# A hybrid encoder layer: opening a second pool of split weights 20 steps into the Q projections

## The chip, the cores and the metric

The kernel runs on one core of a Trainium2 chip. The metric is device time in microseconds (us) for one execution. Five engines matter here: TensorE (PE in the profile, with its weight loads as PEld), VectorE (DVE), ScalarE (ACT), GpSimd (POOL) and SyncE (SP), which issues the DMAs that load weights from device memory.

## The reference

One layer of a bidirectional hybrid encoder over 512 tokens of width 2048, all in float32:

```python
h = rms_norm(x, norm_w)
proj = jnp.einsum('bsd,de->bse', h, w_in)
q, k, v, g_attn, xr, g_lru = jnp.split(proj, SPLITS, axis=-1)
attn_out = attention_group(q, k, v, q_norm_w, k_norm_w)      # 8 heads, 2 KV heads, RoPE, softmax
lru_out = lru_group(xr, conv_w, conv_b, ...)                 # conv, two gates, scans in both directions
mixed = jnp.concatenate([rms_norm(attn_out, attn_norm_w) * jax.nn.silu(g_attn),
                         rms_norm(lru_out, lru_norm_w) * jax.nn.silu(g_lru)], axis=-1)
return x + jnp.einsum('bse,ed->bsd', mixed, w_out)
```

The input projection has 4608 columns: q 1024, k and v 256 each, the attention gate 1024, the LRU input 1024 and the LRU gate 1024.

## The kernel before, in words

**How a projection is done.** A product keeps float32 accuracy by splitting both operands into a high and a low half in a rounded float32 type; `mm3` (L143 to L145) then does three matmuls: high by high, high by low, low by high. The activations `x` are split once at the start and stay. The weights come in *chunks* of 256 rows by 512 columns: one DMA (L192) loads a chunk into a `wr` tile (three buffers), and `wsplit` makes of each 128-row half a pair `wh` (a cast on ACT, L203) and `wl` (a subtraction on DVE, L204). A block of 512 columns takes 8 chunks. In each chunk the projection walks over four output tiles, and each of these four *steps* issues 6 matmuls, 3 for each half of the chunk; so a chunk is 24 matmuls and a block is 32 steps. The Q projections are two such blocks, token-major (`proj_tok`), accumulating in four PSUM tiles `pj`.

**Where the split weights lie.** Pool `xw` always holds four `wh` and four `wl` tiles, two chunks' worth. Where a second pool `wx` is open, it holds four more of each, and `wsplit` alternates:

```python
turn_of[0] += k
pool = pools["wx" if "wx" in pools and turn_of[0] % 2 else "xw"]
```

Since `k` is the half of the chunk (0 or 1), the halves go `xw`, `wx`, then `wx`, `xw`, and so on. A pool that is opened takes space of a pool closed before it, and a tile in it waits for the last use of the old tiles that lay there (`reuse_waits="tile"`). Pools `qkv` and `wx` are opened on the right side just after `lru` was closed there, so they lie on memory of the last LRU tiles.

**The stages around the change.** The LRU projections come first, then the K and V projection, which runs while the second half of the LRU work (`lru_half(1, a2)`, four blocks in two pairs) is done on ACT and DVE. The tail of each pair is a chain: tanh (L421), exp (L427), square root (L431) on ACT; then L434, L435, four scans (L438) and two sums (L443) on DVE. After that the program closes `lru`, opens `rot`, `qkv` and `wx`, and issues the two Q blocks, woven with `kv`: the norm and RoPE of `k` (L491 to L505), the split of `v`, the LRU squares (L448 to L453), the two transposed splits of `k` (`kt`), and the LRU's row scale (L635 on).

**What sets the order.** PE's order is the order in which the code is written (a manual schedule). `weave` runs the generator `kv` and lets the projection advance by as many steps as `kv` yields. The other engines' orders are set by a list scheduler at build time; weight loads and splits have a high priority there (`AHEAD`). On the chip each engine takes its own list in that order.

Of the kernel before, what the change touches and what calls it, by code (L numbers as in the profile page):

```python
# [55 lines left out]
def hybrid_kernel(  # L56
# [27 lines left out]
    def opened(name, side):  # L84
        pools[name] = tc.alloc_tile_pool(name=name, bufs=1, side=side, reuse_waits="tile")
        order[side].append(name)
        return pools[name]
# [18 lines left out]
    def nm(s):  # L106
        cnt[0] += 1
        return f"{s}_{cnt[0]}"
# [30 lines left out]
    def f(ap):  # L139
        return ap.bitcast(F32)  # L140
# [120 lines left out]
    def rows(dst, col, dg):  # L261

        for t in range(NT):
            nc.vector.tensor_scalar(dg[:, t, :], ident, col[:, t : t + 1], None, op0=ALU.mult)
        pb = mm()
        nc.tensor.matmul(pb, ones, dg.rearrange("p t q -> p (t q)"), start=True, stop=True)  # L266
        nc.vector.tensor_copy(dst, pb)
# [177 lines left out]
    def lru_squares():  # L445

        hsum = pools["rot"].tile([P, 2, SEQ], F32, tag="hsum", name="hsum")
        nc.scalar.activation(hsum, hp[0], AF.Square)  # L448
        for pair in hp[1:]:
            yield 2  # L450
            sq = pools["rot"].tile([P, 2, SEQ], F32, tag="hsq", bufs=1, name=nm("hsq"))
            nc.scalar.activation(sq, pair, AF.Square)
            nc.vector.tensor_add(hsum, hsum, sq)  # L453
        sums["l"] = [hsum[:, k, :] for k in range(2)]
# [28 lines left out]
    def norm_rope(es, nh, tab):  # L483

        es = [e[:, : nh * HD].rearrange("p (h d) -> p h d", d=HD) for e in es]
        rs = []
        for e in es:
            r = pools["rot"].tile([P, nh], F32, tag=f"rr{nh}", bufs=NT, name=nm("rr"))
            for h in range(nh):
                sq = pools["rot"].tile([P, HD], F32, tag="sh", bufs=1, name=nm("sh"))  # L490
                nc.scalar.activation(sq, e[:, h, :], AF.Square, accum_out=r[:, h : h + 1])  # L491
            rsqrt_mean(r, r, HD, nh)
            rs.append(r)
        for t, (e, r) in enumerate(zip(es, rs)):
            sq = pools["rot"].tile([P, nh, HD], F32, tag="sq", bufs=2, name=nm("sq"))
            nc.vector.tensor_mul(e, e, r[:, :, None].broadcast_to([P, nh, HD]))
            for s in range(2):
                nc.vector.tensor_mul(
                    sq.rearrange("p h (a s d) -> p h a s d", s=2, d=32)[:, :, :, s, :],
                    e.rearrange("p h (a s d) -> p h a s d", s=2, d=32)[:, :, :, 1 - s, :],  # L500
                    tab[:, t, 1, :].rearrange("p (a s d) -> p a s d", s=2, d=32)[:, None, :, s, :]
                    .broadcast_to([P, nh, 2, 32]),
                )
            nc.vector.tensor_mul(e, e, tab[:, t, 0, :][:, None, :].broadcast_to([P, nh, HD]))
            nc.vector.tensor_add(e, e, sq)  # L505
        return es
# [5 lines left out]
    def turn(rot, h):  # L512

        pt = mm()
        for t in range(NT):
            nc.tensor.transpose(pt[:, t * P : (t + 1) * P], rot[t][:, h, :], ident)  # L516
        return pt

    def split_ps(pt, hi, lo):
        nc.scalar.copy(hi, pt)  # L520
        nc.vector.tensor_sub(lo, pt, f(hi))

    def kv(es):
        rot = norm_rope(es, NKV, rk)
        yield 16
        for t in range(NT):
            vv = es[t][:, NKV * HD :]
            vt = pools["qkv"].tile([P, 2, NKV * HD], F32R, tag="v", bufs=NT, name=nm("v"))
            vh[t], vl[t] = vt[:, 0, :], vt[:, 1, :]
            nc.scalar.copy(vh[t], vv)  # L530
            nc.vector.tensor_sub(vl[t], vv, f(vh[t]))
        yield from lru_squares()
        for h in range(NKV):
            yield (20, 4)[h]
            kt = pools["qkv"].tile([P, 2, SEQ], F32R, tag="kt", bufs=NKV, name=nm("kt"))
            kth[h], ktl[h] = kt[:, 0, :], kt[:, 1, :]
            split_ps(turn(rot, h), kth[h], ktl[h])
        r = group_rstd(sums["l"], "r_l", NB * P)
        yield 4
        rows(gbc, r, pools["rope"].tile([P, NT, P], F32, tag="kv", bufs=NT, name=nm("kv")))  # L540
# [89 lines left out]
    def group_rstd(src, name, n):  # L630

        pr = mm()
        for t in range(NT):
            for k, part in enumerate(src):
                nc.tensor.matmul(  # L635
                    pr[:, t : t + 1], part[:, t * P : (t + 1) * P], ones[:, 0:1],
                    start=k == 0, stop=k == len(src) - 1,
                )
        r = const([P, NT], name)
        nc.vector.tensor_copy(r, pr[:, :NT])  # L640
        rsqrt_mean(r, r, n, NT)
        return r
# [210 lines left out]
    closed("lru")  # L853
    opened("rot", "left")
    opened("qkv", "right")
    opened("wx", "right")
    rots = []

    def q_proj(c0, acc):
# [6 lines left out]

    fill = both()
    weave(fill, kv(kvs))
    drain(fill)

# [128 lines left out]
```

## Time and profile before

| | us |
|---|---|
| median of 3 runs (688.02 to 689.01) | 688.89 |
| the profiled execution | 688.93 |
| its span, first to last instruction | 687.1 |
| PE busy | 663.7 (97%) |
| DVE busy | 486.8 (71%) |
| ACT busy | 332.0 (48%) |
| mean granted TensorE clock | 0.985 |

The span is 1.8 us shorter than the execution's own time. The slices of the page cut the span in 40 equal parts of 17.2 us, each with a digit for the busy tenths of an engine. A matmul's record overlaps the next one's, so what one costs is read from start to start, not from its duration. A row of the timeline ends, in brackets, with the idle time before the instruction and the instruction that ended it.

### The profile page before, as it was taken

Reading aid. Unit: us, or ns where it says so; the run is one execution under the profiler, and the core shown is the slowest. Engines: PE = TensorE matmul, PEld = TensorE weight load, DVE = VectorE, ACT = ScalarE, POOL = GpSimd, SP = SyncE. Lnnn points to the kernel's source line nnn. Section 1 sums busy time; section 2 is a strip of 40 time slices with the busy share of each in tenths; the row PEclk is TensorE's granted clock in tenths of the full one; section 3 lists DMA queues with packets and bytes.
Section 4 is the critical chain, followed back from the end, with each engine's and each line's share of the span. In section 5 each row is a group of like instructions: output and inputs, shape, how many; then the busy total and the mean of one; then the engine's idle time right before and its main releaser. Section 6 shows DMA issues by size and latency. Waiting matters only on the chain.

```text
span 687.1 us, 9526 instructions
## 1 busy us (share of the span) xinstructions
PE 663.7 (97%) x3610; PEld 571.0 (83%) x3610; DVE 486.8 (71%) x819; ACT 332.0 (48%) x581; POOL 57.2 (8%) x77
## 2 busy tenths in 40 slices
PE   8999999998199999999999999999999999999997
PEld 6888888886188887888888888888889989899996
DVE  5878698958782564665685569528989996776944
ACT  4534897599462621654463447425436433242330
POOL 0000000000030310301122222200000000000000
PEclk9999999999599999999999999999999999999999
DMA  8853243221053332132122221232344454372611
GB/s 278 276 154 83 79 123 92 78 76 32 9 175 92 93 92 62 34 95 60 58 62 62 62 62 38 57 91 74 100 129 128 124 182 155 96 242 93 217 60 61
DMA packets 43773, 71.06 MB, mean 103 GB/s; under 512 B 2776, under 2 KB 13136, under 8 KB 43728
## 3 DMA queue, kind: packets, MB, share of 16 engines
q1 hardware_dynamic: 43696, 70.45, 33.6%
q8 instruction: 28, 0.46, 0.3%
q14 instruction: 17, 0.14, 0.1%
q10 hardware_dynamic: 32, 0.01, 0.0%
HBM read 66.25 MB, written 4.19 MB: 103 GB/s over the span
## 4 chain that ended last, share of the span: by engine, by line
PE 95%; ACT 2%; DVE 2%; DMA 1%; issue 0%; SPq 0%; ACTq 0%
PE pj L143 19%; PE pj L144 19%; PE pj L145 19%; PE pj L721 10%; PE mm L721 7%; PE mm L742 6%; PE mm L145 3%; PE mm L143 3%; PE mm L144 3%; PE mm L567 2%; PE mm L229 1%; DMA b<-in_x_dram 1%; DVE b L438 1%; PE mm L516 1%; PE mm L266 0%; ACT b L427 0%
## 5 line engine op out<-in xcount | busy, mean ns | idle before, releaser
L143 PE MATMUL pj<-x,wh 128*128 128x512 f32 x384 | 153.1, 399 | 0.0
L145 PE MATMUL pj<-x,wl 128*128 128x512 f32 x384 | 149.9, 390 | 0.0
L144 PE MATMUL pj<-x,wh 128*128 128x512 f32 x384 | 149.7, 390 | 0.0
L204 DVE TENSOR_TENSOR wl<-wr,wh 128x512 fp32r<-128x512 f32 x144 | 100.8, 717 | 53.2 <-ACT wh L203 53.1
L203 ACT CAST wh<-wr 128x512 fp32r<-128x512 f32 x144 | 86.9, 617 | 104.1 <-PE pj L145 45.6
L143 PE MATMUL pj<-wh,x 128*128 128x512 f32 x192 | 77.2, 402 | 17.2 <-ACT wh L203 17.2
L145 PEld LDWEIGHTS pj<-x,wl 128*128 128x128 f32 x384 | 72.1, 188 | 15.5
L144 PEld LDWEIGHTS pj<-x,wh 128*128 128x128 f32 x384 | 72.3, 188 | 14.0 <-issue 0.5
L143 PEld LDWEIGHTS pj<-x,wh 128*128 128x128 f32 x384 | 72.2, 188 | 13.9 <-issue 0.5
L144 PE MATMUL pj<-wl,x 128*128 128x512 f32 x192 | 76.4, 398 | 0.0
L145 PE MATMUL pj<-wh,x 128*128 128x512 f32 x192 | 76.0, 396 | 0.0
L143 PEld LDWEIGHTS pj<-wh,x 128*128 128x128 f32 x192 | 36.7, 191 | 25.9 <-ACT wh L203 17.6
L721 PE MATMUL pj<-wh,ml 128*128 128x256 f32 x192 | 54.1, 282 | 0.0
L721 PE MATMUL pj<-wh,mh 128*128 128x256 f32 x192 | 54.0, 281 | 0.0
L721 PE MATMUL pj<-wl,mh 128*128 128x256 f32 x192 | 53.8, 280 | 0.0
L678 ACT CAST wh<-wr 128x768 fp32r<-128x768 f32 x24 | 20.1, 837 | 61.6 <-issue 46.4
L569 ACT CAST b<-mm 128x512 fp32r<-128x512 f32 x32 | 18.8, 586 | 59.5 <-PE mm L567 59.5
L555 DVE TENSOR_REDUCE mx<-mm 128x1 f32<-128x512 f32 x32 | 22.0, 688 | 30.8 <-PE mm L145 30.2
L144 PEld LDWEIGHTS pj<-wl,x 128*128 128x128 f32 x192 | 36.6, 191 | 8.6 <-DVE wl L204 0.4
L145 PEld LDWEIGHTS pj<-wh,x 128*128 128x128 f32 x192 | 36.6, 191 | 8.4
L721 PE MATMUL mm<-wh,ml 128*128 128x256 f32 x144 | 40.6, 282 | 0.0
L721 PE MATMUL mm<-wh,mh 128*128 128x256 f32 x144 | 40.5, 281 | 0.0
(203 smaller groups left out, 1320.0 us busy)
## 6 DMA issues: line engine op xcount, KB each, us to landing
wr<-in_w_in_dram SPq DMA_DIRECT2D x71, 512.0 KB, 3.6
wr<-in_w_out_dram SPq DMA_DIRECT2D x32, 512.0 KB, 3.9
xt<-in_x_dram SPq DMA_DIRECT2D x16, 256.0 KB, 4.7
out_dram<-xt SPq DMA_DIRECT2D x15, 256.0 KB, 3.7
b<-in_x_dram SPq DMA_DIRECT2D x7, 512.0 KB, 8.6
k<-in_lru_wa_dram SPq DMA_DIRECT2D x8, 128.0 KB, 5.0
k<-in_lru_wx_dram SPq DMA_DIRECT2D x8, 128.0 KB, 3.2
b<-in_x_dram SPq DMA_DIRECT2D x2, 256.0 KB, 5.1
```

What stands on the lines that cost most here:

```text
L143: nc.tensor.matmul(acc, lh, rh, start=start, stop=False)
L144: nc.tensor.matmul(acc, lh, rl, start=False, stop=False)
L145: nc.tensor.matmul(acc, ll, rh, start=False, stop=stop)
L203: nc.scalar.copy(hi, raw[:, k, :])
L204: nc.vector.tensor_sub(lo, raw[:, k, :], f(hi))
L229: nc.tensor.transpose(pt[:, t * P : (t + 1) * P], xc[:, t, ks], ident)
L555: nc.vector.tensor_reduce(mx, sc, axis=AX.X, op=ALU.max, negate=True)
L567: nc.tensor.transpose(pt[:, s * P : (s + 1) * P], p[:, s * P : (s + 1) * P], ident)
L569: nc.scalar.copy(pth[:, :, tt], p3)
L678: nc.scalar.copy(hi[:, to], part)
L721: nc.tensor.matmul(dst, lh[:, a, ts_], rh[:, b_, :], start=bank in fresh, stop=last and s == 1 and rh is bh and lh is al, skip_group_check ...
L742: nc.tensor.matmul(dst, lh[:, a, ts_], rh[:, w], start=new, stop=last and k == 1 and j == 2, skip_group_check=True,)
```

## The change

`wx` is opened later: no longer between the K/V projection and the Q projections, but from within `kv`, after the Q projections have advanced 20 steps (five chunks of the first block). The first yield of `kv` grows from 16 to 20 steps and a later one shrinks from 20 to 16, so the two `kt` transposes stand at the same steps as before (42 and 46); the split of `v` and the four LRU squares come four steps later in the code.

```diff
     def kv(es):
         rot = norm_rope(es, NKV, rk)
-        yield 16
+        yield 20
+        opened("wx", "right")
         for t in range(NT):
...
         yield from lru_squares()
         for h in range(NKV):
-            yield (20, 4)[h]
+            yield (16, 4)[h]
...
     closed("lru")
     opened("rot", "left")
     opened("qkv", "right")
-    opened("wx", "right")
     rots = []
```

No instruction is added or removed. PE's, POOL's and SP's orders are the same instructions in the same places, apart from the names of buffers. ACT's and DVE's orders differ between the end of the K/V projection and the end of the first Q block. Two places show it. In the names, `wr_1723`, `wr_1757` and `wr_1791` are Q chunks 0, 1 and 2 of before; a chunk's first half has the lower number (`wh_1725`, then `wh_1729` for chunk 0; `wh_1759` and `wh_1763` for chunk 1; `wh_1793` and `wh_1797` for chunk 2). In the changed kernel chunks 0 to 4 are `wr_1720`, `wr_1754`, `wr_1788`, `wr_1822` and `wr_1856`, and chunks 5 to 7 are `wr_1907`, `wr_1947` and `wr_1984`. The `b` tiles belong to the last LRU pair.

ACT, from the K/V projection's last evacuation on. Before:

```order
L479 ACTIVATE kv_1632<-pj_1212,rstd 128x512
L203 CAST wh_1793<-wr_1791 128x512
L427 ACTIVATE b_287_1506<-b_287_1506,c_92 128x512
L427 ACTIVATE b_298_1569<-b_298_1569,c_92 128x512 x2
L431 ACT_TABLE_LOAD
L431 ACTIVATE b_313_1634<-b_313_1634 128x1024
L431 ACTIVATE b_314_1637<-b_314_1637 128x1024
L203 CAST wh_1729<-wr_1723 128x512
L203 CAST wh_1759<-wr_1757 128x512
L203 CAST wh_1797<-wr_1791 128x512
L491 ACTIVATE sh_1668,rr_1667<-kv_1626 128x128
```

With the change:

```order
L203 CAST wh_1756<-wr_1754 128x512
L203 CAST wh_1760<-wr_1754 128x512
L427 ACTIVATE b_287_1506<-b_287_1506,c_92 128x512
L427 ACTIVATE b_298_1569<-b_298_1569,c_92 128x512 x2
L431 ACT_TABLE_LOAD
L431 ACTIVATE b_313_1634<-b_313_1634 128x1024
L203 CAST wh_1790<-wr_1788 128x512
L203 CAST wh_1794<-wr_1788 128x512
L431 ACTIVATE b_314_1637<-b_314_1637 128x1024
L203 CAST wh_1824<-wr_1822 128x512
L203 CAST wh_1828<-wr_1822 128x512
L203 CAST wh_1858<-wr_1856 128x512
```

Before, the second half of chunk 0 (`wh_1729`) was cast behind both square roots; with the change chunk 0 was cast in full earlier (its two casts take the places that `wh_1725` and `wh_1763` had before), and chunks 1 to 4 are cast in order, with the square roots between them.

DVE, over the same part. Before:

```order
L204 TENSOR_TENSOR wl_1794<-wr_1791,wh_1793 128x512
L434 SCALAR_TENSOR_TENSOR b_313_1634<-b_287_1506,b_313_1634 128x1024
L434 SCALAR_TENSOR_TENSOR b_314_1637<-b_298_1569,b_314_1637 128x1024
L435 TENSOR_TENSOR b_288_1507<-b_288_1507,b_313_1634 128x1024
L435 TENSOR_TENSOR b_299_1570<-b_299_1570,b_314_1637 128x1024
L438 SCALAR_TENSOR_TENSOR b_288_1507<-b_287_1506,b_288_1507 128x512 x2
L438 SCALAR_TENSOR_TENSOR b_299_1570<-b_298_1569,b_299_1570 128x512
L443 TENSOR_TENSOR hs_1650<-b_288_1507 128x512
L438 SCALAR_TENSOR_TENSOR b_299_1570<-b_298_1569,b_299_1570 128x512
L443 TENSOR_TENSOR hs_1650<-b_299_1570 128x512
L204 TENSOR_TENSOR wl_1730<-wr_1723,wh_1729 128x512
L204 TENSOR_TENSOR wl_1760<-wr_1757,wh_1759 128x512
```

With the change:

```order
L434 SCALAR_TENSOR_TENSOR b_313_1634<-b_287_1506,b_313_1634 128x1024
L204 TENSOR_TENSOR wl_1791<-wr_1788,wh_1790 128x512
L204 TENSOR_TENSOR wl_1795<-wr_1788,wh_1794 128x512
L435 TENSOR_TENSOR b_288_1507<-b_288_1507,b_313_1634 128x1024
L434 SCALAR_TENSOR_TENSOR b_314_1637<-b_298_1569,b_314_1637 128x1024
L204 TENSOR_TENSOR wl_1825<-wr_1822,wh_1824 128x512
L204 TENSOR_TENSOR wl_1829<-wr_1822,wh_1828 128x512
L438 SCALAR_TENSOR_TENSOR b_288_1507<-b_287_1506,b_288_1507 128x512 x2
L435 TENSOR_TENSOR b_299_1570<-b_299_1570,b_314_1637 128x1024
L443 TENSOR_TENSOR hs_1650<-b_288_1507 128x512
L438 SCALAR_TENSOR_TENSOR b_299_1570<-b_298_1569,b_299_1570 128x512
L204 TENSOR_TENSOR wl_1859<-wr_1856,wh_1858 128x512
```

Before, the whole tail of the LRU pair stood ahead of the second halves of chunks 0, 1 and 2; with the change the subtractions of chunks 2, 3 and 4 stand between its instructions. Behind the last row of the changed list come `wl_1863`, the last scan, the last L443, and then chunk 5's first half, `wl_1910`, whose cast `wh_1909` is the first in `wx`.

## The prediction

> **What bounds the kernel now.** I read the page's head and its slices first, then the waits, the chain and the stretch around the one dip.
>
> ```profile
> span 687.1 us, 9526 instructions
> PE 663.7 (97%) x3610; PEld 571.0 (83%) x3610; DVE 486.8 (71%) x819; ACT 332.0 (48%) x581; POOL 57.2 (8%) x77
> ...
> PE   8999999998199999999999999999999999999997
> ...
> PEclk9999999999599999999999999999999999999999
> ```
>
> TensorE is busy 97% of the span, so almost anything that lets it run earlier shortens the kernel by as much. One slice, the eleventh, has PE at 1 and the granted clock at 5. TensorE's own waits name it:
>
> ```profile
> PE pj L143 <- ACT wh L203: 17.2, 1, 17.2
> PE mm L229 <- DMA b<-in_x_dram: 1.5, 1, 1.5
> ```
>
> One wait of 17.2 us, for a cast of a weight half on ACT (L203). The rest of PE's idle time, 687.1 − 663.7 − 17.2 = 6.2 us, lies at the two ends, where the slices show an 8 and a 7. The chain of waits shows what that cast waited for (start, us, what):
>
> ```profile
> 173.88 1.06 ACT b L431
> 174.97 2.36 DVE b L434 x2
> ...
> 184.72 0.70 DVE hs L443
> 185.44 0.63 ACT wh L203
> 186.11 0.79 PE pj L143
> ```
>
> So the chain leaves TensorE and runs through the end of the last LRU pair (square root, L434, L435, the scans L438, the sum L443); one cast later TensorE goes on. Its timeline on both sides of the gap (start, us, line, form):
>
> ```profile
> 168.53 0.39 PE L145 MATMUL pj<-wh,x 128*128 128x512 f32 x1
> 186.11 0.79 PE L143 MATMUL pj<-wh,x 128*128 128x512 f32 x1 [17.20 <-ACT wh L203]
> 186.84 0.79 PE L144 MATMUL pj<-wl,x 128*128 128x512 f32 x1
> ...
> 191.62 0.40 PE L143 MATMUL pj<-wh,x 128*128 128x512 f32 x1
> ...
> 246.43 0.60 PE L516 MATMUL mm<-ident,kv 128*128 128x128 f32 x4
> ```
>
> The matmul at 168.53 is the third of the Q projections (three on the first half `wh_1725`); the fourth needs `wh_1729`, the first tile in the second pool `wx`. From 168.53 to 191.62 are 13 starts. At 191.62 stands Q matmul 16, and the first `kt` transpose at 246.43 comes after 42 steps = 252 matmuls, so at full clock one costs (246.43 − 191.62)/237 = 0.231 us. ACT's timeline shows which instructions stood ahead of that cast:
>
> ```profile
> 159.37 1.31 ACT L203 CAST wh<-wr 128x512 fp32r<-128x512 f32 x2 [0.60 <-PE pj L145]
> ...
> 170.12 0.60 ACT L203 CAST wh<-wr 128x512 fp32r<-128x512 f32 x1
> 170.62 1.95 ACT L427 ACTIVATE b<-b,c 128x512 f32<-128x512 f32 x3
> 172.59 1.28 ACT L431 ACT_TABLE_LOAD   x1
> 173.88 2.00 ACT L431 ACTIVATE b<-b 128x1024 f32<-128x1024 f32 x2
> 185.44 1.66 ACT L203 CAST wh<-wr 128x512 fp32r<-128x512 f32 x3 [9.56 <-DVE hs L443]
> ```
>
> By the ACT order before, the two casts at 159.37 are `wh_1725` and `wh_1763`, the one at 170.12 is `wh_1793` (all in `xw`), and the three at 185.44 are the ones in `wx`. ACT was done at 175.9 and stood 9.56 us, with the data loaded: what was missing was the place to write to. `wx` lies where the LRU pool's tiles lay, and its first tile comes free with the last L443. The stretches say the same (length, then busy us of PE, PEld, DVE, ACT, POOL, the granted clock, DMA share, GB/s):
>
> ```profile
> 140.00:168.90 28.90, 28.90 (x127) 23.47 (x126) 21.53 (x26) 28.06 (x41) 0.00 (x0) 1.00 0.19 56
> 168.90:186.10 17.20, 0.02 (x1) 0.00 (x0) 11.11 (x12) 7.60 (x12) 0.00 (x0) 0.56 0.00 0
> 186.10:191.70 5.60, 5.59 (x13) 4.15 (x14) 4.74 (x13) 5.60 (x19) 2.10 (x4) 0.52 0.63 211
> 191.70:228.50 36.80, 36.80 (x161) 29.89 (x160) 18.38 (x34) 12.82 (x24) 3.99 (x4) 1.00 0.37 111
> ```
>
> In the gap DVE has 6.1 us and ACT 9.6 us free, and no DMA runs. The first row matters as much: to 168.9 the KV projections ran from `xw` alone, with its four slots, beside LRU work, and PE lacked nothing.
>
> **The change part by part.** *Removed:* the wait of Q chunk 0 for `wx`. With `wx` closed for 20 steps (5 chunks of 4), both halves of chunk 0 go to `xw`, and `wh_1726` stands where `wh_1763` stood, in the pair at 159.37. So chunk 0 is ready in full at about 163.4, before PE needs it.
>
> What this is worth, if nothing takes its place: 191.62 − 168.53 = 23.09 us for 13 starts that cost 13 × 0.231 = 3.01 us at full clock. That is **20.1 us**: 17.35 of standing and 2.75 because 12 matmuls after it ran at 0.43 us or more (granted clock 0.52 in the third row). The profiled execution took 688.93 us (span 687.1, 1.8 around it), 0.04 above the median of 688.89.
>
> The Trainium skill, "TensorE: Matmul & The Clock Gate", Part 1, says that a clock once dropped returns after about 3.4 us of activity, and that the number of slow matmuls varies from run to run; an estimate by it, half of 3.4, is 1.7 us for the ramp and would make the sum 19.1. The trace has 12 slow ones and 2.75 us, and that is what I take.
>
> *Moved:* the splits of chunks 1 to 4. They must now come in time among the LRU instructions, so each is worked forward through the new ACT and DVE orders. The DVE rows give the prices:
>
> ```profile
> 162.19 1.26 DVE L204 TENSOR_TENSOR wl<-wr,wh 128x512 fp32r<-128x512 f32 x2
> ...
> 170.75 0.69 DVE L204 TENSOR_TENSOR wl<-wr,wh 128x512 fp32r<-128x512 f32 x1 [2.70 <-ACT wh L203]
> 174.97 2.36 DVE L434 SCALAR_TENSOR_TENSOR b<-b,b 128x1024 f32<-128x1024 f32 x2 [3.52 <-ACT b L431]
> 177.25 2.35 DVE L435 TENSOR_TENSOR b<-b,b 128x1024 f32<-128x1024 f32 x2
> 179.52 3.45 DVE L438 TENSOR_TENSOR_SCAN b<-b,b 128x512 f32<-128x512 f32 x3
> 182.88 0.67 DVE L443 TENSOR_TENSOR hs<-b 128x512 f32<-128x512 f32 x1
> 183.47 1.22 DVE L438 TENSOR_TENSOR_SCAN b<-b,b 128x512 f32<-128x512 f32 x1
> ```
>
> From start to start that is 0.60 for a `wl` or an L443, 1.14 for an L434, L435 or scan; on ACT about 0.52 for a cast, 0.62 for an L427, 1.0 for an L431. PE starts Q two matmuls before 168.53, at 168.07, and needs a chunk every 24 × 0.231 = 5.55 us.
>
> - Chunk 1, needed at 173.6: casts at 170.12 and 170.64, `wl` done at 171.4 and 172.1. Margin 1.5.
> - Chunk 2, needed at 179.2: on ACT three L427 and the table load end at 174.4, one L431 at 175.4, then the two casts to 176.5 (their slots were free at 173.6). On DVE one L434 to 176.6, then both `wl` to 177.9. Margin 1.3.
> - Chunk 3, needed at 184.7: its casts wait for PE to leave chunk 1's slots, 178.5 and 179.2, and end at 179.9; on DVE L435 and L434 end at 180.2, `wl` at 181.4. Margin 3.3.
> - Chunk 4, needed at 190.3: casts when chunk 2 is left, 184.7, done at 185.4; DVE has two scans, L435, L443 and a scan first, to 186.4, `wl` at 187.7. Margin 2.6.
> - Chunk 5, needed at 195.8, is the first with a half in `wx`. The last L443 ends at 189.4, that half is ready at 190.9; its other half, behind the first `sh` and `v` instructions, at 194.4. Margin 1.4.
>
> So no stall: the gap's free time is the cover. Without it the price would be the missing margin, chunk by chunk: with every ACT and DVE instruction 10% longer the same working still gives no stall, with 20% longer 2.2 us, nearly all of it at chunk 5. Both ends go into the range; I take 0, as the durations are of this stage.
>
> *DMAs:* the loads keep their order on SP; each needs the `wl` of three chunks before.
>
> ```profile
> DMA to landing us min/median/max: 3.6/3.7/5.5
> ```
>
> Chunk 3's load is issued at 163.4 and landed by 168.9 at the latest, its cast is at 178; chunk 4's is issued at 172.1, landed by 177.6, cast at 184; chunk 5's by 183.4, cast at 189.5. Nothing queues.
>
> *What is late next:* the LRU's end slips from 185.4 to 189.4, and behind it the `v` split (four steps later, four casts and four subtractions), `k`'s norm and the LRU squares. Before, they ended here, and were needed by PE at 246.43 and 252.88:
>
> ```profile
> 200.12 0.42 DVE L505 TENSOR_TENSOR kv<-kv,sq 128x256 f32<-128x256 f32 x1
> ...
> 203.40 1.23 DVE L453 TENSOR_TENSOR hsum<-hsum,hsq 128x1024 f32<-128x1024 f32 x1 [0.52 <-ACT hsq L452]
> ...
> 252.88 1.84 PE L635 MATMUL mm<-ones,hsum 128*128 128x1 f32 x16
> ```
>
> Now they end near 209, and PE is there at 226.3 and 232.8. Margins 17 and 23 us: free. PE's order is unchanged, and from the second Q block on so are ACT's and DVE's, so everything behind moves forward as one.
>
> Sum: 688.93 − 20.1 = **668.8 us**; the median of the runs shown gives the same.
>
> **The rivals.**
>
> *Small stalls stay.* Margins of 1.3 to 1.5 us are thin, and every split sits in a queue with LRU work. For it: DVE would be nearly full from 175 to 196. Against it: the KV row, 28.90 of 28.90 under the same arrangement. By the 20% case, 2.2 us: 671.0; and if a single stall grew long enough to drop the clock, 2.75 more: 673.8.
>
> *The clock's share does not come back.* The 2.75 us of slow matmuls could turn up elsewhere, if the clock dips in another place when PE never rests. Against it: clock 1.00 in the rows on both sides. 688.93 − 17.35 = 671.6.
>
> *The ring of four becomes the bound, and it gets slower.* Chunks 2 to 5 can only be split once PE has left the slots, so from slot to matmul there is one chunk, 5.55 us; a cast that waits for PE also holds up the LRU's and `k`'s work behind it. The trace shows such holding: the cast at 185.44 stood 9.56 us. The longest DVE block ahead of a pair is about 5.2 us; with 1.2 for the pair and 0.6 for the cast, a chunk that met all of it would come 1.5 us late, 6 us over four chunks: 674.8. It decides for slower only from 5 us per chunk on, 20.1 in all, over 688.9, for instance if `wx` were released after 195.8 + 20.1 = 215.9 instead of 189.4. No row has such a delay. The Trainium skill, same page, "Architectural detail", calls ACT and DVE strict FIFO; the trace agrees, since nothing passed the cast that stood.
>
> *It does not do what it says:* the casts come early, but PE waits for the same release all the same. 688.9. Against it: the wait of the fourth matmul is gone from its place, with its operand now in the pair at 159.37.
>
> **How the numbers follow.** Forecast 0.80, its own range 667.5 to 670.5 (the pitch, and 0.1% of spread between runs). Small stalls 0.12. Clock 0.05. Ring, slower than before, 0.015. No effect 0.015. The range for 8 in 10 runs from 666.8 (2 us below, the spread from 688.02 to 689.01 taken twice) to 672.8, which takes in the clock's 671.6 and the 20% case. A measurement of this kernel can tell about 0.2% from no change, 1.4 us. Faster: 0.80 + 0.12 + 0.05 = 0.97; within 0.2%: 0.015; slower: 0.015.
>
> **What would show it.** In the changed kernel PE's waits no longer hold a row of 17 us; Q starts near 168 without a gap; the eleventh slice has PE and PEclk at 9; L443's last end is near 189; the first `kt` transposes stand near 226. A wait of PE on L203 or L204 between 173 and 200 would show the stalls, its place by chunk (5 first). It is wrong if the span is over 671 or if PE rests anywhere else.

## The result: 668.28 us against 688.52, and the profile after

The changed kernel takes 668.28 us (median of 4 runs, 667.91 to 668.66), the kernel before 688.52 in the same comparison: a ratio of 0.9706, interval 0.9689 to 0.9723, 20.2 us less. The forecast was 668.8. The page's head and slices of the changed kernel:

```profile
span 666.5 us, 9524 instructions
PE 660.7 (99%) x3610; PEld 569.6 (85%) x3610; DVE 486.1 (73%) x819; ACT 331.1 (50%) x581; POOL 56.8 (9%) x77
...
PE   8999999999999999999999999999999999999997
...
PEclk9999999999999999999999999999999999999999
```

The dip of the eleventh slice is gone from both rows, and the span is 20.6 us shorter. PE's waits are two, both in the first 10 us:

```profile
PE mm L802 <- POOL ones L151: 1.1, 1, 1.1
PE mm L229 <- DMA b<-in_x_dram: 0.9, 1, 0.9
```

The same stretches as before, without PE's gap (length, busy us of PE, PEld, DVE, ACT, POOL, clock, DMA share, GB/s):

```profile
168.90:186.10 17.20, 17.20 (x77) 14.24 (x77) 11.92 (x14) 11.02 (x16) 0.00 (x0) 1.00 0.34 92
186.10:191.70 5.60, 5.60 (x27) 4.63 (x26) 4.88 (x8) 2.14 (x8) 0.00 (x1) 1.00 0.32 94
191.70:228.50 36.80, 36.80 (x163) 30.00 (x162) 31.01 (x64) 24.35 (x72) 12.22 (x16) 1.00 0.38 115
```

In the 17.2 us in which PE stood, it now works at full clock, the weight DMAs run, and DVE does hardly more than before (11.9 us against 11.1). In the last of these stretches DVE and ACT now have more to do than before (31.0 us against 18.4, and 24.4 against 12.8), as what follows the first Q block comes forward with PE. PE's timeline of the changed kernel: the third Q matmul, the first of chunk 5 (Q matmul 121), and the first `kt` transpose (252 Q matmuls done):

```profile
168.51 0.39 PE L145 MATMUL pj<-wh,x 128*128 128x512 f32 x1
...
195.26 0.40 PE L143 MATMUL pj<-wh,x 128*128 128x512 f32 x1
...
225.77 0.60 PE L516 MATMUL mm<-ident,kv 128*128 128x128 f32 x4
```

The transposes come 20.66 us earlier than the 246.43 of before, and nothing of that is lost or gained behind them: the last matmul of the program starts 20.65 us earlier too. How the splits came in time is read from ACT's and DVE's timelines.

```profile
170.10 1.13 ACT L203 CAST wh<-wr 128x512 fp32r<-128x512 f32 x2
...
175.34 1.13 ACT L203 CAST wh<-wr 128x512 fp32r<-128x512 f32 x2
176.38 1.05 ACT L431 ACTIVATE b<-b 128x1024 f32<-128x1024 f32 x1
178.46 1.31 ACT L203 CAST wh<-wr 128x512 fp32r<-128x512 f32 x2 [1.02 <-PE pj L145]
183.90 1.31 ACT L203 CAST wh<-wr 128x512 fp32r<-128x512 f32 x2 [4.13 <-PE pj L145]
189.56 1.15 ACT L203 CAST wh<-wr 128x512 fp32r<-128x512 f32 x2 [4.36 <-DVE hs L443]
```

```profile
170.74 1.29 DVE L204 TENSOR_TENSOR wl<-wr,wh 128x512 fp32r<-128x512 f32 x2 [2.71 <-ACT wh L203]
...
176.61 1.29 DVE L204 TENSOR_TENSOR wl<-wr,wh 128x512 fp32r<-128x512 f32 x2
...
180.09 1.29 DVE L204 TENSOR_TENSOR wl<-wr,wh 128x512 fp32r<-128x512 f32 x2
...
186.39 1.27 DVE L204 TENSOR_TENSOR wl<-wr,wh 128x512 fp32r<-128x512 f32 x2
...
188.83 0.69 DVE L443 TENSOR_TENSOR hs<-b 128x512 f32<-128x512 f32 x1
...
205.00 0.42 DVE L505 TENSOR_TENSOR kv<-kv,sq 128x256 f32<-128x256 f32 x1
...
208.57 1.23 DVE L453 TENSOR_TENSOR hsum<-hsum,hsq 128x1024 f32<-128x1024 f32 x1 [0.53 <-ACT hsq L452]
```

The last cast row still waits for the last L443, 4.36 us: the wait for `wx` is not gone, it has moved to chunk 5, where PE arrives at 195.26 and does not feel it.

### The profile page after: what moved, and what is told of

It is laid out like the page before. It is cut to its first block, busy times and chain, and to the rows that moved or that the text cites. A ratio compares the mean times of both kernels' runs of the same rounds, so it can differ in the third digit from the quotient of the medians.

```text
span 666.5 us, 9524 instructions
## 1 busy us (share of the span) xinstructions
PE 660.7 (99%) x3610; PEld 569.6 (85%) x3610; DVE 486.1 (73%) x819; ACT 331.1 (50%) x581; POOL 56.8 (9%) x77
## 4 chain that ended last, share of the span: by engine, by line
PE 98%; DMA 1%; SPq 0%; DVE 0%; issue 0%
PE pj L143 20%; PE pj L145 20%; PE pj L144 20%; PE pj L722 10%; PE mm L722 8%; PE mm L743 6%; PE mm L145 3%; PE mm L143 3%; PE mm L144 3%; PE mm L568 2%; DMA b<-in_x_dram 1%; PE mm L229 1%; PE mm L516 1%; PE mm L266 0%; PE mm L636 0%; PE pj L743 0%
## 5 line engine op out<-in xcount | busy, mean ns | idle before, releaser
L143 PE MATMUL pj<-wh,x 128*128 128x512 f32 x192 | 75.9, 395 | 0.0
L145 PE MATMUL pj<-wh,x 128*128 128x512 f32 x192 | 75.0, 391 | 0.0
L679 ACT CAST wh<-wr 128x768 fp32r<-128x768 f32 x24 | 20.1, 836 | 60.9 <-issue 46.2
```

The source lines that it names most:

```text
L143: nc.tensor.matmul(acc, lh, rh, start=start, stop=False)
L145: nc.tensor.matmul(acc, ll, rh, start=False, stop=stop)
L679: nc.scalar.copy(hi[:, to], part)
```

## The experiments

Theory: PE stood because chunk 0's second half was to be written where the last LRU pair still lived, and for no other reason. The rivals were the other half of the edit (the split of `v` and the squares four steps later), the order of the casts on ACT, and, for the size, what the clock had to do with it. Each kernel was measured beside the kernel before.

**One half of the edit at a time.** First the choice of the pool alone:

```diff
-    turn_of = [0]
+    turn_of, hold = [0], [0]
...
-        pool = pools["wx" if "wx" in pools and turn_of[0] % 2 else "xw"]
+        pool = pools["wx" if "wx" in pools and turn_of[0] % 2 and not hold[0] else "xw"]
+        hold[0] = max(0, hold[0] - 1)
...
     opened("wx", "right")
+    hold[0] = 10
```

> The kernel before, with wx opened where it was and the yields as they were; only the choice of the pool is changed: the first ten halves (Q chunks 0 to 4) go to xw. My theory (the gap is the wait of chunk 0's second half for memory of the last LRU tiles, and nothing else): PE's 17.2 us row is gone, L443 ends near 189.5, time 668.3 +- 1. Rival (moving the split of v and the LRU squares by four steps is what freed ACT and DVE): the gap stays, 688.5.

Measured 668.52 us, ratio 0.9713 (0.9700 to 0.9726); PE has no wait but the two at the start:

```profile
PE mm L802 <- POOL ones L151: 1.1, 1, 1.1
PE mm L230 <- DMA b<-in_x_dram: 0.4, 1, 0.4
```

Then the yields alone:

```diff
-        yield 16
+        yield 20
...
-            yield (20, 4)[h]
+            yield (16, 4)[h]
```

> The kernel before with the other part alone: the yields 20 and 16, wx opened where it was. My theory: nothing changes on the path, PE waits 17.2 us as before, 688.5 +- 1. Rival (the yields): 668 to 675.

One run, 688.52 us. PE's waits in it:

```profile
PE pj L143 <- ACT wh L203: 17.2, 1, 17.2
```

The choice of the pool is the whole gain; the yields by themselves are worth nothing that one run would show. Both as the theory had it.

**The memory itself.** Here the second set of slots is used from the first Q chunk on, as before, but taken from the ring that the attention outputs use only later:

```diff
-        pool = pools["wx" if "wx" in pools and turn_of[0] % 2 else "xw"]
+        if "qkv" in pools and "rope" in pools and turn_of[0] % 2:
+            hi, lo = (aring.tile([P, SEQ], F32R, name=nm(n)) for n in ("wh", "wl"))
+        else:
+            hi = pools["xw"].tile([P, SEQ], F32R, tag="wh", bufs=4, name=nm("wh"))
+            lo = pools["xw"].tile([P, SEQ], F32R, tag="wl", bufs=4, name=nm("wl"))
...
-    opened("wx", "right")
```

> As the kernel before in time (the second set of four slots is used from the first Q chunk on), but the slots lie in the ring that the attention outputs take later, memory that no LRU tile held. My theory (memory, not the moment): no gap, within 1 us of 668.3. Rival (casts for a second set of slots come behind the LRU's square roots on ACT, whatever memory they write): the 17 us wait stays, 685 or more. On the matmul's rate: if 0.2313 belongs to any second set of slots, all 384 Q matmuls have it, 668.8; if it belongs to the place of wx, 0.2272 throughout, 667.2.

669.15 us, ratio 0.9718 (0.9705 to 0.9732), no wait of PE. So neither using a second set from the first chunk on nor having one is at fault, which leaves the memory. The build placed the casts for these slots ahead of the square roots, so the ACT order changed with it and this run alone does not part the two; the next ones do. The 0.9 us over the changed kernel's 668.28 come up again further down.

**Opening at other steps.** With 8 and 12 steps, chunks 0 and 1 are cast ahead of the square roots as with 20 steps. The diff is that for 8; for 12 the yields are 12 and 24.

```diff
-        yield 20
+        yield 8
         opened("wx", "right")
...
-            yield (16, 4)[h]
+            yield (28, 4)[h]
```

> The changed kernel, but wx opened after 8 steps (two chunks) instead of 20, the later yield 28 instead of 16. My theory (PE stands whenever it needs a tile of wx before the LRU's last L443, and its clock drops with it): chunk 2 starts at 178.9 and its second half waits for a cast at about 187.6; a gap of some 8.7 us after the third matmul of chunk 2, then about 12 slow matmuls, 2.75 us: 668.3 + 8.7 + 2.75 = 679.7. Rival (the order of casts on ACT, not the memory: chunk 0 and 1 cast ahead of the square roots is enough): 668.3 to 670.

681.37 us in one run. PE's wait, and ACT's cast that ended it:

```profile
PE pj L143 <- ACT wh L203: 8.7, 1, 8.7
```

```profile
189.26 1.67 ACT L203 CAST wh<-wr 128x512 fp32r<-128x512 f32 x3 [8.69 <-DVE hs L443]
```

> The same with wx opened after 12 steps (three chunks). My theory: chunk 3 starts at 184.4 and its first half is the one in wx, cast at about 188.9 and usable at 189.6: a gap of about 5.2 us at the first matmul of chunk 3. 673.5 if the clock outlasts a gap of 5 us, 676.2 if it drops as after the 17 us. Rival (order of casts): 668.3 to 670.

676.64 us in one run:

```profile
PE pj L143 <- ACT wh L203: 5.1, 1, 5.1
```

```profile
188.65 1.67 ACT L203 CAST wh<-wr 128x512 fp32r<-128x512 f32 x3 [4.43 <-DVE hs L443]
```

The gaps are where and as long as worked out (8.7 and 5.2 us), and in both the cast waits for the last L443. Wherever the first tile of `wx` is wanted before that, PE stands until it; the order of casts is out as a cause. The clock dropped after the 5.1 us gap too, so the higher of the two figures for 12 steps held. The run with 8 steps is 1.7 us over its figure; its trace shows a start-up 1.5 us longer than that of the changed kernel, in work that is the same in both: the clock records have full clock from 10.4 us on, those of the changed kernel from 4.7 us on.

**The clock's part.** Dummy matmuls that nobody reads fill the gap of the kernel before; `keep` is 140 in one kernel and 152 in the other for the first Q block, and 0 elsewhere:

```diff
                     mm3(acc[t], lh[kk][:, ts_], ll[kk][:, ts_], wh, wl, kk == 0, kk == nk - 1)
+                    if keep and c == t == k == 0:
+                        dummy = mm()
+                        for _ in range(keep):
+                            nc.tensor.matmul(dummy[:, : 2 * P], wv[:, :P], wv, start=True, stop=True)
...
```

> The kernel before, with 140 bfloat16 matmuls of 256 columns between the third and the fourth Q matmul, written to a PSUM tile that nobody reads; at about 0.107 us each they fill 15 of the 17.4 us of the gap. They change neither the wait nor what is computed. My theory (2.75 us of the gain are the clock alone, which dropped because PE stood): Q goes on at 186.1 as before but at once with 0.23 us per matmul, 685.8. Rival (the 12 slow matmuls are slow because their operands come late): 688.5.

This missed: 688.28 us over ten runs from 685.87 to 688.72, ratio 0.999 (0.9979 to 1.0001). From start to start a dummy took 0.109 us, close to the 0.107 that I had set; but 140 of them end at 184.6, and that left PE standing:

```profile
PE pj L143 <- ACT wh L203: 1.9, 1, 1.9
...
PE pj L144 <- DVE wl L204: 0.2, 1, 0.2
```

In the traced run the clock dropped all the same, as the stretches show:

```profile
180.00:184.50 4.50, 4.50 (x42) 3.83 (x40) 4.50 (x5) 0.00 (x0) 0.00 (x0) 1.00 0.00 0
...
187.20:190.30 3.10, 3.10 (x8) 2.46 (x8) 2.24 (x6) 3.10 (x16) 1.56 (x4) 0.51 0.64 183
```

The ten runs fall into two groups by their mean granted clock: six with 0.996 or 0.997 took 688.23 to 688.72 us, and four with 0.999 or 1.000 took 685.87 to 687.26. The traced run is one of the six. One half-speed period as long as its own, 3.41 us, lowers the mean by 0.0025, so the four can hardly have had one behind the gap. The medians of the two groups, 688.62 and 687.01, are 1.6 us apart: the experiment took the drop away in four runs of ten, and these put its price at some 1.6 us, close to half of 3.41. With 152:

> The kernel before with 152 dummy matmuls in the gap instead of 140. With 140 they ended at 184.6, PE stood 1.9 us, and eight matmuls after it were slow. At 0.115 us each 152 end at 185.9 and leave some 0.2 us. Theory (the clock alone): Q goes on at 186.1 to 186.4 with 0.23 us per matmul, clock 1.00 throughout, 685.8 and no spread over 1 us. Rival (operands): still eight or more slow matmuls, 688.3.

686.81 us (686.60 to 686.90), ratio 0.9966 (0.9954 to 0.9979): 2.3 us less, between 1.4 and 3.2. The dummies ended at 185.6, not at 185.9 as expected, since the 0.115 us set there for each was too high. The same stretch as before, now at full clock, and PE's timeline after the gap:

```profile
186.10:191.70 5.60, 5.27 (x22) 4.09 (x23) 4.65 (x12) 5.60 (x20) 2.10 (x4) 1.00 0.67 214
```

```profile
186.20 0.50 PE L143 MATMUL pj<-wh,x 128*128 128x512 f32 x1 [0.59 <-ACT wh L203]
186.93 0.50 PE L144 MATMUL pj<-wl,x 128*128 128x512 f32 x1 [0.23 <-DVE wl L204]
187.27 0.40 PE L145 MATMUL pj<-wh,x 128*128 128x512 f32 x1
187.50 0.39 PE L143 MATMUL pj<-wh,x 128*128 128x512 f32 x1
```

The first start-to-start is still 0.73 us and the second 0.34, where 0.23 is usual: there PE waits for the `wl` that DVE makes after the cast. That is 0.6 us that no clock explains. The rest of the 2.75 us that the profiled run of before lost, 2.1, was the clock.

**Is `wx` needed at all?** The line that opens it is left out:

```diff
-    opened("wx", "right")
```

> wx is never opened: all 16 Q chunks go through the four slots of xw; yields as before the change. My theory says that no gap opens at chunk 0, so at most 668.3 plus what the four slots cost later. Rival A (the four slots are too few beside the norm and RoPE of Q, which load ACT and DVE from 208 on): stalls in the second Q block, 670 to 675. Rival B, from the two traces: PE's matmuls start every 0.2313 us where wx is in use and every 0.2272 us where xw alone is; if that belongs to wx, the 264 Q matmuls after step 20 save 0.0041 us each, 1.1 us: 667.2.

667.23 us, ratio 0.9686 (0.9673 to 0.9699). The four slots of `xw` are enough for the whole of Q; PE waits nowhere but at the start. Since its interval overlaps that of the changed kernel, both ran once more in the same rounds.

> The changed kernel again, to stand beside the one that never opens wx in the same rounds: 668.3.

> The kernel that never opens wx again: if wx after step 20 does nothing but slow the matmuls that read from it, 1.1 us below the changed kernel, 667.2; if the first comparison was chance, the same as the changed kernel.

668.53 us (667.92 to 668.60) against 667.36 us (666.60 to 667.65), 1.2 us apart. The intervals of the two ratios still overlap a little, but the single runs do so in neither comparison, and the timelines below show where the difference arises. The version without `wx` beats both kernels.

**Where the 1.2 us are.** Two more kernels change where the Q splits lie. In the first, all of them go to the attention ring (the diff is against the kernel of *The memory itself*); in the second, the choice is held for ten halves as in the first experiment and `wx` is opened on the left (against the kernel before):

```diff
-        if "qkv" in pools and "rope" in pools and turn_of[0] % 2:
+        if "qkv" in pools and "rope" in pools:
...
-    opened("rot", "left")
-    opened("qkv", "right")
-    opened("wx", "right")
+    opened("wx", "left")
+    opened("rot", "left")
+    opened("qkv", "right")
...
```

> All splits of the Q projections go to the attention outputs' ring (four slots, at 212 to 229 KB of a partition) and none to xw (86 to 103 KB). For the matmul's rate. Theory P (place: a moving operand read from there costs 0.234 us instead of 0.227): all 384 Q matmuls slow, 384 x 0.0069 = 2.7 us over the 667.2 of the kernel that never opens wx: 669.9, starts 0.234 apart. Theory A (alternation between two distant places costs it): 0.227 throughout, 667.2. Neither expects a gap at chunk 0, since no LRU tile lay there.

> As the changed kernel in time (the first ten halves in xw, then two sets of slots in turn), but the second set lies at 119 to 136 KB of a partition instead of 145 to 162. The kernels so far had 0.227 us per matmul at 86 to 103 KB and 0.234 at 145 to 162 and at 212 to 229 KB. If the change lies below 119 KB: 0.2313 after step 20 as in the changed kernel, 668.3. If it lies above 136 KB: 0.2272, 667.2. If it lies between (the four wh slots at 119 to 127 KB, the wl slots at 127 to 136 KB): the matmuls that read wl from there alone are slow, 0.228, about 667.4.

669.89 us (ratio 0.9726, 0.9710 to 0.9743) and 667.09 us (0.9679, 0.9665 to 0.9694). PE's timeline gives the rate without any wait in it: from the start of the last gate matmul ahead of the K/V projection's last chunk to that of the first `kt` transpose are 277 starts, 252 of them of Q matmuls. The changed kernel (repeat), no `wx`, the second set in the ring, all in the ring, `wx` on the left:

```profile
162.60 0.40 PE L145 MATMUL mm<-k,k 128*128 128x512 f32 x1
...
226.02 0.60 PE L516 MATMUL mm<-ident,kv 128*128 128x128 f32 x4
```

```profile
162.83 0.40 PE L145 MATMUL mm<-k,k 128*128 128x512 f32 x1
...
225.66 0.60 PE L516 MATMUL mm<-ident,kv 128*128 128x128 f32 x4
```

```profile
162.81 0.40 PE L145 MATMUL mm<-k,k 128*128 128x512 f32 x1
...
226.78 0.60 PE L518 MATMUL mm<-ident,kv 128*128 128x128 f32 x4
```

```profile
162.86 0.40 PE L145 MATMUL mm<-k,k 128*128 128x512 f32 x1
...
227.36 0.60 PE L518 MATMUL mm<-ident,kv 128*128 128x128 f32 x4
```

```profile
162.35 0.40 PE L145 MATMUL mm<-k,k 128*128 128x512 f32 x1
...
225.18 0.60 PE L517 MATMUL mm<-ident,kv 128*128 128x128 f32 x4
```

That is 63.42, 62.83, 63.97, 64.50 and 62.83 us. Against no `wx`, the changed kernel pays 0.59 us for 132 matmuls after step 20, the ring as second set 1.14 for 252, the ring alone 1.67 for 252, `wx` on the left nothing. Alternation alone is out: the kernel with all splits in the ring does not alternate and is the slowest, and the one with `wx` on the left alternates and loses nothing. The place of the operand counts. It is not the whole account, though: both kernels that take half of the splits from `wx` on the right or from the ring pay 0.0045 us per matmul (0.59/132 and 1.14/252), two thirds and not half of the 0.0066 of the ring alone. Whether going to and fro between two places far apart adds to the price was not tested.

## Why the prediction was right

*What bounds.* As read: PE's gap of 17.2 us, ended by the last L443 through one cast. The first two experiments and the two steps put the cause on the tile's memory, not on the order around it.

*The sum.* Forecast 17.35 of standing and 2.75 behind it, 20.1; measured 20.66 at the `kt` transposes and 20.2 between medians. The 17.35 holds. The 2.75 holds as a total for the profiled run, but "granted clock" was said of all of it: the clock is 2.1 of it, and 0.6 is the wait for the first `wl`. The estimate from the Trainium skill, 1.7 us for the ramp ("TensorE: Matmul & The Clock Gate", Part 1), is nearer to the clock's own 2.1 than 2.75 was. What is missing, 0.57 us, is a term that I had in front of me and did not price: I took 0.231 us for every Q matmul, while the K/V projection's row stood at 0.228. The 13 starts and the 237 behind them now run 57.26 us (168.51 to 225.77) where 250 × 0.2313 would be 57.8, because chunks 0 to 4 are read from `xw` alone. That the medians are only 0.1 us from the forecast 20.1 is in part luck. The 2.75 came from one profile, and what follows a gap differs from run to run: with the yields alone, where PE stands for the same 17.2 us, the 13 starts took 22.54 us instead of 23.09. A share of the clock that was high for the typical run can so have made up for the term left out.

*The moved splits.* The working through ACT and DVE held to 0.1 us up to chunk 4: both halves ready at 172.0, 177.9, 181.4 and 187.7, as forecast; last L443 189.5 against 189.4. No chunk came late. What is late next was as harmless as said: `k`'s norm ended at 205.4 and the squares at 209.8, for matmuls at 225.8 and 232.2.

*The rivals.* No stall appeared, so the 12% for small stalls went unused; the granted clock stayed at 1.00, so the clock's share did come back; and the ring of four is far from being a bound: it serves all 16 chunks without a wait. The fear that more splits in four slots could cost something had the sign the wrong way round: it is the second pool, where it lay, that costs.

*The chances.* The case taken as the likeliest came about, within its own range of 667.5 to 670.5; the range of 6 us was wider than the working needed.

## What to carry to other kernels

When one engine stands for long at the start of a stage, ask which memory the first tile of that stage takes over and who used it last; a later first use is as good as free memory, provided that the other slots feed the engine until then. Work the queues of the engines in between forward from the durations of the rows, instruction by instruction: that gave the ready times of chunks 1 to 4 here to 0.1 us. And before a buffer is moved, measure whether it is needed: without the second pool the kernel is 1.2 us faster than with it opened late on the right.

## What the runs showed of the hardware that was not expected

**A matmul's rate depends on where its moving operand lies.** By the addresses of the build, `xw` has its weight slots at 86 to 103 KB of a partition (thousands of bytes), `wx` on the left at 119 to 136, `wx` on the right at 145 to 162 and the ring at 213 to 229. Read from the first two, matmuls of 128x512 start every 0.227 us (62.83/277); from the ring alone every 0.233 (1.67/252 more); where half of them come from the ring or from `wx` on the right, the mean is 0.231. Whether it is the address, the distance to the stationary `x` tiles (21 to 87 KB) or what else is read and written nearby is open; no run here moved one without the others.

**The clock can drop after a short gap, and does not always.** In the traced run with 140 dummies a stand of 1.9 us (with 0.2 more after one matmul) was followed by granted clock 0.51; with 152 dummies one of 0.6 us was not. The clock records show the half-speed period around the gap as 3.41 us (140 dummies), 6.83 (opening at 12 steps), 10.24 (at 8 steps), 17.07 (yields alone) and 20.48 (before), all multiples of 3.41; the Trainium skill ("TensorE: Matmul & The Clock Gate", Part 1) names a free-running window of that length, and the trace agrees. So whether a short gap drops the clock, and what a gap costs behind it, would depend on where in a window it falls. That fits the two groups of the kernel with 140 dummies; but only one of its runs has a trace, so where the window lay in the other nine is not shown.
